# Stick-breaking attention: the second term of the scores contracted over 128 rows, the keys' low part in both halves

## The chip, the cores and the metric

The kernel runs on one core of a Trainium2 chip. The metric is the device time of one execution in microseconds (us); lower is better. Engines are named as in the profile: PE (TensorE) multiplies matrices, and PEld is its loading of the stationary operand; DVE is VectorE, ACT is ScalarE, POOL is GpSimd; SP issues the DMAs.

## The reference

One layer of a hybrid encoder on 1024 tokens with 1024 features, in float32: one input projection feeds an HGRN2 recurrence (4 heads of 128) and a stick-breaking attention (8 heads of 64); both are projected, gated, summed and projected again; then come a layer norm, a gated feed-forward part with a short causal convolution, a per-layer embedding and a second layer norm. The change concerns the attention:

```python
def stick_breaking_attention(q, k, v):
    qh = jnp.transpose(q, (0, 2, 1, 3)) * (Dh ** -0.5)
    ...
    def block(args):
        z = jnp.einsum('bhtd,bhsd->bhts', qi, kh).astype(jnp.float32)
        mask = (key_pos[None, :] < t_pos[:, None])[None, None]
        log_fail = jnp.where(mask, jax.nn.log_sigmoid(-z), 0.0)
        suffix = lax.cumsum(log_fail, axis=3, reverse=True) - log_fail
        log_w = jnp.where(mask, jax.nn.log_sigmoid(z) + suffix, 0.0)
        w = jnp.where(mask, jnp.exp(log_w), 0.0)
        return jnp.einsum('bhts,bhsd->bhtd', w, vh)
```

## The kernel before

Values are split into a high part of type fp32r and a low part, the difference (`split`: ACT copies, DVE subtracts). A product of two split matrices takes three matmuls, high by high, high by low and low by high (`mm3`, lines 93 to 95).

**Projections as filler.** The input projections are cut into small pieces (`add_fm`, `add_tm`, `add_qk0`); `fill` puts as many of them on PE between two attention steps as a balance of the remaining work says. PE's order up to the end of the input projections is that of the code (`manual_schedule`). The orders of the other engines are made by a scheduler when the program is built, and each engine works strictly in its order.

**Attention.** The 8 heads are worked in 4 pairs p; heads hd = 0 and 1 of a pair lie in partitions 0 to 63 and 64 to 127 of the projections. `q_out` (from line 316) writes for each head a tile of 128 partitions with the query's high part in one half and its low part in the other: `qsa` for hd 0, `qsb` for hd 1. `k_out` (from line 328) writes for each pair and each half h of the tokens, from the bank `psk`: `kca` and `kcb`, the high part of the keys of hd 0 and of hd 1, each in both halves of the partitions (ACT writes one half, DVE copies it to the other), and `kl`, the low part, hd 0 in the lower and hd 1 in the upper half (DVE).

`sb_weights` then makes the scores z of 128 queries with 128 to 1024 keys, in pieces of at most 512 columns:

```python
            mm(z[:, :s1 - s0], lhsT=qs[:, ts], rhs=kc[:, s0:s1], start=True, stop=False)
            mm(z[:, :s1 - s0], lhsT=qs[r, ts], rhs=kl[r, s0:s1], start=False, stop=True)
```

Line 383 contracts over 128 rows (the query's high and low part with the keys' high part), line 384 over the 64 rows `r` (the query's high with the keys' low part). Such a couple is called a pair of z matmuls here; there are 96. Behind it ACT makes two sigmoids, `f` (line 385) and `be` (386); DVE masks `f` (389) and takes its running product (391); POOL masks `be` (390) and multiplies it by `f` (393). `sb_apply` transposes `be` on PE (`tr`, 409), splits it into `wth` (ACT, 79) and `wtl` (DVE, 80), and multiplies both by the values into `av` (420); DVE adds the result to `ob` (436). `stick_breaking` runs 32 steps (4 pairs, 2 heads, 4 blocks of 256 queries), the scores of one step interleaved with the application of the step before.

`load_w` brings a weight tile by DMA and splits it (ACT line 87, DVE line 89). All larger work tiles come from the pool `gp` (24 buffers, `G(...)`); the tiles of z and `tr` from four PSUM banks (`Z`).

Of the kernel before, what the change touches and what calls it, by code (L numbers as in the profile page):

```python
# [7 lines left out]
F32 = mybir.dt.float32  # L8
F32R = mybir.dt.float32r
U8 = mybir.dt.uint8  # L10
AF = mybir.ActivationFunctionType
ALU = mybir.AluOpType
# [23 lines left out]
def layer_kernel(ctx, tc, xT, pT, w_in, w_a, w_b, w_out, w_up, w_down, w_pe, w_pg,  # L36
                 cols, conv, sbm, hgm, idn, g2r, b2r, outT, outR):
    nc = tc.nc
    cst = ctx.enter_context(tc.tile_pool(name="cst", bufs=1))
    xp = ctx.enter_context(tc.tile_pool(name="xp", bufs=16))  # L40
    wp = ctx.enter_context(tc.tile_pool(name="wp", bufs=2))
    gp = ctx.enter_context(tc.tile_pool(name="gp", bufs=24))
    hp = ctx.enter_context(tc.tile_pool(name="hp", bufs=6))
    sm = ctx.enter_context(tc.tile_pool(name="sm", bufs=4))
    
# [9 lines left out]
    def G(name, dt=F32, shape=None):  # L55
        return gp.tile(shape or [P, T], dt, tag="g", name=name)
# [19 lines left out]
    mm = nc.tensor.matmul  # L76
# [38 lines left out]
    for c, nm in ((16, "q0"), (20, "k0")):  # L115
        raw = wp.tile([P, T], F32, tag="wr", name="wr_" + nm)
        hi = wp.tile([P, T], F32R, tag="wh", name="wh_" + nm, bufs=3)
        lo = wp.tile([P, T], F32R, tag="wl", name="wl_" + nm, bufs=3)
# [64 lines left out]

    XH, XL = (lambda k: xh[k]), (lambda k: xl[k])

# [1 line left out]
    jobs = []  # L187
    state = {"job": 0, "chunk": 0, "credit": 0.0}
    CH = 0.65
# [118 lines left out]
            i += 1  # L308
        return n * CH

# [1 line left out]
    qk = [None] * 4  # L312
    v2 = [None] * 4
    ob = [None] * 4
# [13 lines left out]
    def k_out(p):  # L328
        def evac(psk, h, c):
            if h == 0:  # L330
                qk[p] = qk[p] + (G(f"kca{p}", F32R), G(f"kcb{p}", F32R), G(f"kl{p}", F32R))
            ka, kb, kl = qk[p][2:]
            nc.scalar.copy(out=ka[0:64, c], in_=psk[0:64])
            nc.vector.tensor_copy(out=ka[64:128, c], in_=ka[0:64, c].bitcast(F32))
            nc.vector.tensor_tensor(out=kl[0:64, c], in0=psk[0:64], in1=ka[0:64, c].bitcast(F32), op=ALU.subtract)
            nc.scalar.copy(out=kb[64:128, c], in_=psk[64:128])
            nc.vector.tensor_copy(out=kb[0:64, c], in_=kb[64:128, c].bitcast(F32))
            nc.vector.tensor_tensor(out=kl[64:128, c], in0=psk[64:128], in1=kb[64:128, c].bitcast(F32), op=ALU.subtract)

        return evac  # L340

# [23 lines left out]
    def sb_names(p, hd):  # L365
        r = slice(0, 64) if hd == 0 else slice(64, 128)
        ro = slice(64, 128) if hd == 0 else slice(0, 64)
        return r, ro, f"{p}{hd}"

    def sb_weights(p, hd, tb, ws):  # L370
        r, ro, nm = sb_names(p, hd)
        qa, qb, ka, kb, kl = qk[p]
        qs, kc = (qa, ka) if hd == 0 else (qb, kb)
        if hd == 0 and tb == 0:
            ob[p] = G(f"ob{p}")
        W = (tb + 1) * P
        ts = slice(tb * P, tb * P + P)
        f = G(f"f{nm}{tb}")
        be = G(f"be{nm}{tb}")
        for s0 in range(0, W, 512):  # L380
            s1 = min(s0 + 512, W)
            z = Z(f"z{nm}{tb}{s0}")
            mm(z[:, :s1 - s0], lhsT=qs[:, ts], rhs=kc[:, s0:s1], start=True, stop=False)
            mm(z[:, :s1 - s0], lhsT=qs[r, ts], rhs=kl[r, s0:s1], start=False, stop=True)  # L384
            nc.scalar.activation(f[:, s0:s1], z[:, :s1 - s0], AF.Sigmoid, scale=-0.125)
            nc.scalar.activation(be[:, s0:s1], z[:, :s1 - s0], AF.Sigmoid, scale=0.125)  # L386
            if s1 < W:
                yield
        nc.vector.tensor_tensor(out=f[:, ts], in0=f[:, ts], in1=msb[:, 1, :], op=ALU.max)
        nc.gpsimd.tensor_tensor(out=be[:, ts], in0=be[:, ts], in1=msb[:, 0, :], op=ALU.mult)  # L390
        nc.vector.tensor_tensor_scan(out=f[:, :W][:, ::-1], data0=f[:, :W][:, ::-1], data1=f[:, :W][:, ::-1],  # L391
                                     initial=1.0, op0=ALU.mult, op1=ALU.bypass)
        nc.gpsimd.tensor_tensor(out=be[:, :W - 1], in0=be[:, :W - 1], in1=f[:, 1:W], op=ALU.mult)  # L393
        ws.append(be)
        yield
# [67 lines left out]
        for _ in sb_apply(*prev):  # L463
            fill(1.3)

# [1 line left out]
    va, sga = [None] * 2, [None] * 2  # L467
    oa = [None] * 4

# [48 lines left out]
        add_fm(h, f"hq{h}", evac_q)  # L518
        add_fm(4 + h, f"hf{h}", evac_f)

    # the keys of an odd block of 128 tokens lie in falling order within every 32 of them
    def key_rows(kt, tot, m):
        k5 = kt.rearrange("p (c e t) -> p c e t", c=4, e=2)
        t5 = tot.rearrange("p (c e g) -> p c e g", c=4, e=2)
# [172 lines left out]
                    fill(left(("ia1", "ga1", "gb0", "gb3")[h]) * w / max(rest, w))  # L697
                    rest -= w

# [1 line left out]
    def split4(src, name):  # L701
        hs, ls = [], []
        for k in range(4):
# [65 lines left out]

            yproj(j, u, mh, ml, f"ya{j}", out)  # L770

# [1 line left out]
    def ln_gen(get, c0, n, emit, name):  # L773
        cs = slice(c0, c0 + n)
        nb = n // P
# [37 lines left out]
            nc.vector.tensor_tensor(out=get(j)[:, cs], in0=get(j)[:, cs], in1=pr[:, :n], op=ALU.mult)  # L813
            emit(j, cs)

# [1 line left out]
    add_qk0([w[2:] for w in wqk], (q_out(0), k_out(0)))  # L817
    add_vb(0), add_q(1), add_k(1)
    add_vb(1), add_q(2), add_k(2)
# [15 lines left out]
    R = lambda j: rt[j]  # L835
# [27 lines left out]

    X1H, X1L = (lambda k: x1h[k]), (lambda k: x1l[k])

# [1 line left out]
    def split_p(hi, lo, src):  # L867
        nc.scalar.copy(out=hi, in_=src)
        nc.gpsimd.tensor_tensor(out=lo, in0=src, in1=hi.bitcast(F32), op=ALU.subtract)
# [125 lines left out]
    with tc.manual_schedule(engines={mybir.EngineType.PE}):  # L995
# [5 lines left out]
        for i in range(4):  # L1001
            src, lst, nm = ((pT[i], pp, f"p{i}") if i < 2 else (w_pe[i - 2], pe_u, f"pe{i}"))
# [41 lines left out]
    for bs in groups:  # L1044
        last = bs is groups[-1]
# [90 lines left out]
                nc.vector.tensor_tensor(out=r, in0=r, in1=self.pr[:, :Q], op=ALU.mult)  # L1136
                y_emit(j, self.cs, how[j], cuts)

    # the last tokens lie over the partitions, with R transposed into the sums
    class Rows:  # L1140
        def __init__(self, i):
            self.i, self.nm = i, f"rw{i}"
# [170 lines left out]
```

## Time and profile before

| | us |
|---|---|
| median of 3 runs | 1756.48 (1752.68 to 1758.9) |
| the profiled execution, first to last instruction (the page gives no other time for it) | 1753.0 |
| PE busy | 1720.5 |
| DVE busy | 1025.1 |
| ACT busy | 585.7 |
| POOL busy | 373.8 |

The profiled execution is one of its own; it lies 3.5 us under the median of the runs and within their range. Neighbouring PE rows overlap, as matmuls are pipelined and their ends are modelled. What a matmul costs in a stream is the distance from its start to the next start. The attention takes the stretch from about 28 to 366 us. Its view by windows gives busy time by engine, the granted clock of PE (1.00 is full) and DMA.

### The profile page before, as it was taken

The numbers are of one execution on the slowest core, as the hardware profiler recorded it, in microseconds if no ns is written. First come the engines' busy times: TensorE is split into PE (matmuls) and PEld (weight loads), VectorE is DVE, ScalarE is ACT, GpSimd is POOL, SyncE is SP. The second block draws the span as 40 slices with busy tenths as digits, with TensorE's granted clock in tenths as the row PEclk, the third lists the DMA queues.
The fourth block names the chain that finished last, engine by engine and source line by source line (L and its number), as shares of the span: only waits on it lengthen the run. The fifth ranks groups of instructions, "written<-read, shape, count | busy, mean of one in ns | idle before, by whom it ended". The sixth has DMA issues, their size and how long they took to land.

```text
span 1753.0 us, 21252 instructions
## 1 busy us (share of the span) xinstructions
PE 1720.5 (98%) x8660; PEld 1437.9 (82%) x8660; DVE 1025.1 (58%) x1463; ACT 585.7 (33%) x899; POOL 373.8 (21%) x293
## 2 busy tenths in 40 slices
PE   8999999999999999999999999999999999999997
PEld 6778778789988888887788888888888888888896
DVE  6677867776576423347776326456456456456465
ACT  5455555542233221222345112222222222222233
POOL 0344434431012000005540102012012012012043
PEclk9999999999999999999999999999999999999998
DMA  5000000100011111111421210120120121121102
GB/s 198 25 25 25 25 25 25 37 25 29 33 37 36 49 42 55 37 60 57 148 73 36 73 36 24 49 73 24 49 72 27 47 73 34 39 72 37 60 25 96
DMA packets 26977, 88.11 MB, mean 50 GB/s; under 512 B 2944, under 2 KB 5632, under 8 KB 26880
## 3 DMA queue, kind: packets, MB, share of 16 engines
q1 hardware_dynamic: 26880, 86.76, 14.8%
q8 instruction: 68, 1.11, 0.3%
q14 instruction: 29, 0.24, 0.0%
HBM read 82.55 MB, written 4.19 MB: 49 GB/s over the span
## 4 chain that ended last, share of the span: by engine, by line
PE 87%; DVE 8%; ACT 2%; issue 1%; POOL 1%; DMA 1%; POOLq 0%; SPq 0%; ACTq 0%; DVEq 0%
PE uv L93 4%; PE uv L95 4%; PE ug L94 4%; PE ug L93 4%; PE uv L94 4%; PE ug L95 4%; PE d L94 4%; PE d L93 4%; PE d L95 4%; PE z L384 2%; PE pi_gb L95 2%; PE pi_gb L93 2%; DVE f L391 2%; PE pg L93 2%; PE pg L95 2%; PE pi_gb L94 2%
## 5 line engine op out<-in xcount | busy, mean ns | idle before, releaser
L906 POOL TENSOR_TENSOR cuv<-cuv,cug 128x1024 f32<-128x1024 f32 x21 | 50.4, 2400 | 552.2 <-DVE cug L888 552.2
L93 PE MATMUL uv<-x1h,wh_uv 128*128 128x512 f32 x352 | 136.9, 389 | 0.0
L95 PE MATMUL uv<-x1h,wl_uv 128*128 128x512 f32 x352 | 136.9, 389 | 0.0
L94 PE MATMUL uv<-x1l,wh_uv 128*128 128x512 f32 x352 | 136.9, 389 | 0.0
L93 PE MATMUL ug<-x1h,wh_ug 128*128 128x512 f32 x352 | 136.9, 389 | 0.0
L94 PE MATMUL ug<-x1l,wh_ug 128*128 128x512 f32 x352 | 136.9, 389 | 0.0
L95 PE MATMUL ug<-x1h,wl_ug 128*128 128x512 f32 x352 | 136.9, 389 | 0.0
L93 PE MATMUL d<-gh,hd 128*128 128x512 f32 x288 | 112.0, 389 | 0.0
L94 PE MATMUL d<-gl,hd 128*128 128x512 f32 x288 | 112.0, 389 | 0.0
L95 PE MATMUL d<-gh,ld 128*128 128x512 f32 x288 | 112.0, 389 | 0.0
L887 DVE SCALAR_TENSOR_TENSOR cug<-ug,cv,cug 128x1023 f32<-128x1023 f32 x21 | 26.9, 1282 | 134.1 <-ACT cug L886 134.1
L955 DVE TENSOR_TENSOR r<-r,d 128x512 f32<-128x512 f32 x144 | 94.3, 680 | 11.6 <-PE d L95 11.6
L390 POOL TENSOR_TENSOR be<-be,msb 128x128 f32<-128x128 f32 x64 | 64.4, 1007 | 170.2 <-ACT be L386 170.2
L391 DVE TENSOR_TENSOR_SCAN f<-f 128x128 f32<-128x128 f32 (+3 forms) x64 | 93.8, 1466 | 2.0
L393 POOL TENSOR_TENSOR be<-be,f 128x127 f32<-128x127 f32 (+3 forms) x64 | 77.2, 1207 | 56.3 <-DVE f L391 50.7
L886 ACT ACTIVATE cug<-ug,cv 128x1024 f32<-128x1024 f32 x21 | 25.3, 1206 | 160.3 <-PE ug L95 160.3
L95 PEld LDWEIGHTS uv<-x1h,wl_uv 128*128 128x128 f32 x352 | 66.1, 188 | 13.8
L94 PEld LDWEIGHTS ug<-x1l,wh_ug 128*128 128x128 f32 x352 | 66.1, 188 | 13.7
L94 PEld LDWEIGHTS uv<-x1l,wh_uv 128*128 128x128 f32 x352 | 66.1, 188 | 13.7
L95 PEld LDWEIGHTS ug<-x1h,wl_ug 128*128 128x128 f32 x352 | 66.1, 188 | 13.7
L93 PEld LDWEIGHTS ug<-x1h,wh_ug 128*128 128x128 f32 x352 | 66.1, 188 | 13.7
L93 PEld LDWEIGHTS uv<-x1h,wh_uv 128*128 128x128 f32 x352 | 66.1, 188 | 13.6
(462 smaller groups left out, 4617.0 us busy)
## 6 DMA issues: line engine op xcount, KB each, us to landing
wr_uv<-in_w_up SPq DMA_DIRECT2D x22, 512.0 KB, 3.2
wr_ug<-in_w_up SPq DMA_DIRECT2D x22, 512.0 KB, 3.2
wr_d<-in_w_down SPq DMA_DIRECT2D x21, 512.0 KB, 3.3
wr_wo<-in_w_out SPq DMA_DIRECT2D x16, 512.0 KB, 3.3
wr_gb<-in_w_in SPq DMA_DIRECT2D x8, 512.0 KB, 3.3
wr_gt<-in_w_in SPq DMA_DIRECT2D x8, 512.0 KB, 3.2
wr_pg<-in_w_pg SPq DMA_DIRECT2D x8, 512.0 KB, 3.3
xr<-in_xT SPq DMA_DIRECT2D x7, 512.0 KB, 8.8
```

Source lines behind the costliest of these rows:

```text
L93: mm(ps, lhsT=ah, rhs=bh, start=start, stop=False)
L94: mm(ps, lhsT=ah, rhs=bl, start=False, stop=False)
L95: mm(ps, lhsT=al, rhs=bh, start=False, stop=stop)
L384: mm(z[:, :s1 - s0], lhsT=qs[r, ts], rhs=kl[r, s0:s1], start=False, stop=True)
L390: nc.gpsimd.tensor_tensor(out=be[:, ts], in0=be[:, ts], in1=msb[:, 0, :], op=ALU.mult)
L391: nc.vector.tensor_tensor_scan(out=f[:, :W][:, ::-1], data0=f[:, :W][:, ::-1], data1=f[:, :W][:, ::-1], initial=1.0, op0=ALU.mult, op1=ALU ...
L393: nc.gpsimd.tensor_tensor(out=be[:, :W - 1], in0=be[:, :W - 1], in1=f[:, 1:W], op=ALU.mult)
L886: nc.scalar.activation(o, ps, AF.Identity, bias=cv[:, c, 3:4], scale=cv[:, c, 2:3])
L887: nc.vector.scalar_tensor_tensor(out=o[:, 1:], in0=ps[:, :T - 1], scalar=cv[:, c, 1:2], in1=o[:, 1:], op0=ALU.mult, op1=ALU.add)
L906: nc.gpsimd.tensor_tensor(out=val, in0=val, in1=gt, op=ALU.mult)
L955: nc.vector.tensor_tensor(out=R(j)[:, cs], in0=R(j)[:, cs], in1=ps[:, :n], op=ALU.add)
```

## The change

The low part of the keys gets one tile per head, `kla` and `klb`, in which it stands in both halves of the partitions; line 384 contracts over all 128 rows. The product has one more term by this (query's low by keys' low part). Each of the 8 calls of `k_out`'s `evac` so issues four subtractions on DVE in place of two. The pool `gp` gets 27 buffers; the program is built with a `dynamic_dma_scratch_size` of 1024. Comments that went are left out below.

```diff
-    gp = ctx.enter_context(tc.tile_pool(name="gp", bufs=24))
+    gp = ctx.enter_context(tc.tile_pool(name="gp", bufs=27))
...
     def k_out(p):
         def evac(psk, h, c):
             if h == 0:
-                qk[p] = qk[p] + (G(f"kca{p}", F32R), G(f"kcb{p}", F32R), G(f"kl{p}", F32R))
-            ka, kb, kl = qk[p][2:]
-            nc.scalar.copy(out=ka[0:64, c], in_=psk[0:64])
-            nc.vector.tensor_copy(out=ka[64:128, c], in_=ka[0:64, c].bitcast(F32))
-            nc.vector.tensor_tensor(out=kl[0:64, c], in0=psk[0:64], in1=ka[0:64, c].bitcast(F32), op=ALU.subtract)
-            nc.scalar.copy(out=kb[64:128, c], in_=psk[64:128])
-            nc.vector.tensor_copy(out=kb[0:64, c], in_=kb[64:128, c].bitcast(F32))
-            nc.vector.tensor_tensor(out=kl[64:128, c], in0=psk[64:128], in1=kb[64:128, c].bitcast(F32), op=ALU.subtract)
+                qk[p] = qk[p] + tuple(G(f"{nm}{p}", F32R) for nm in ("kca", "kcb", "kla", "klb"))
+            ka, kb, la, lb_ = qk[p][2:]
+
+            for hi, lo, r, ro in ((ka, la, slice(0, 64), slice(64, 128)), (kb, lb_, slice(64, 128), slice(0, 64))):
+                nc.scalar.copy(out=hi[r, c], in_=psk[r])
+                nc.vector.tensor_copy(out=hi[ro, c], in_=hi[r, c].bitcast(F32))
+                for o in (r, ro):
+                    nc.vector.tensor_tensor(out=lo[o, c], in0=psk[r], in1=hi[r, c].bitcast(F32), op=ALU.subtract)
...
-        qa, qb, ka, kb, kl = qk[p]
-        qs, kc = (qa, ka) if hd == 0 else (qb, kb)
+        qa, qb, ka, kb, la, lb_ = qk[p]
+        qs, kc, kl = (qa, ka, la) if hd == 0 else (qb, kb, lb_)
...
-            mm(z[:, :s1 - s0], lhsT=qs[r, ts], rhs=kl[r, s0:s1], start=False, stop=True)
+            mm(z[:, :s1 - s0], lhsT=qs[:, ts], rhs=kl[:, s0:s1], start=False, stop=True)
...
-    nc = bacc.Bacc("TRN2", target_bir_lowering=False, num_devices=1)
+    nc = bacc.Bacc("TRN2", target_bir_lowering=False, num_devices=1, dynamic_dma_scratch_size=1024)
```

PE's order is the same before and after, line by line. DVE's order changes around the keys. The first place is the beginning of the attention, where the first queries and keys are written (numbers at tile names are those of buffers; the running product of line 391 is named SCALAR_TENSOR_TENSOR). Before:

```order
L334 CAST kca_311<-kca_311 64x512
L335 TENSOR_TENSOR kl_313<-pi_qk_195,kca_311 64x512
L324 TENSOR_TENSOR qsb_302<-pi_qk_191,qsb_302 64x512
L334 CAST kca_311<-kca_311 64x512
L337 CAST kcb_312<-kcb_312 64x512
L338 TENSOR_TENSOR kl_313<-pi_qk_195,kcb_312 64x512
L335 TENSOR_TENSOR kl_313<-pi_qk_199,kca_311 64x512
L89 TENSOR_TENSOR wl_q_336<-wr_q_333,wh_q_335 128x512 x2
L337 CAST kcb_312<-kcb_312 64x512
L338 TENSOR_TENSOR kl_313<-pi_qk_199,kcb_312 64x512
L389 TENSOR_TENSOR f_359<-f_359,msb 128x128
```

With the change:

```order
L336 CAST kca_311<-kca_311 64x512
L338 TENSOR_TENSOR kla_313<-pi_qk_195,kca_311 64x512
L324 TENSOR_TENSOR qsb_302<-pi_qk_191,qsb_302 64x512
L338 TENSOR_TENSOR kla_313<-pi_qk_195,kca_311 64x512
L336 CAST kca_311<-kca_311 64x512
L338 TENSOR_TENSOR kla_313<-pi_qk_199,kca_311 64x512
L336 CAST kcb_312<-kcb_312 64x512
L338 TENSOR_TENSOR klb_314<-pi_qk_195,kcb_312 64x512 x2
L338 TENSOR_TENSOR kla_313<-pi_qk_199,kca_311 64x512
L89 TENSOR_TENSOR wl_q_341<-wr_q_338,wh_q_340 128x512 x2
L336 CAST kcb_312<-kcb_312 64x512
L338 TENSOR_TENSOR klb_314<-pi_qk_199,kcb_312 64x512 x2
```

Eight subtractions stand where four stood, all ahead of the first mask of `f` (line 389). The second place is where the keys of pair 1 are finished (second half of the tokens), just as the scores of that pair begin. Before:

```order
L335 TENSOR_TENSOR kl_1022<-pi_k_1036,kca_1020 64x512
L89 TENSOR_TENSOR wl_q_1144<-wr_q_1141,wh_q_1143 128x512
L337 CAST kcb_1021<-kcb_1021 64x512
L338 TENSOR_TENSOR kl_1022<-pi_k_1036,kcb_1021 64x512
L436 TENSOR_TENSOR ob_358<-av_1062,avt_1158 64x256
L389 TENSOR_TENSOR f_1168<-f_1168,msb 128x128
L391 SCALAR_TENSOR_TENSOR f_1168<-f_1168 128x128
L389 TENSOR_TENSOR f_1185<-f_1185,msb 128x128
L391 SCALAR_TENSOR_TENSOR f_1185<-f_1185 128x256
L80 TENSOR_TENSOR wtl_1209<-tr_1203,wth_1208 128x512
```

With the change:

```order
L338 TENSOR_TENSOR kla_1027<-pi_k_1044,kca_1025 64x512 x2
L89 TENSOR_TENSOR wl_q_1154<-wr_q_1151,wh_q_1153 128x512
L436 TENSOR_TENSOR ob_363<-av_1070,avt_1168 64x256
L336 CAST kcb_1026<-kcb_1026 64x512
L338 TENSOR_TENSOR klb_1028<-pi_k_1044,kcb_1026 64x512 x2
L389 TENSOR_TENSOR f_1178<-f_1178,msb 128x128
L389 TENSOR_TENSOR f_1195<-f_1195,msb 128x128
L391 SCALAR_TENSOR_TENSOR f_1178<-f_1178 128x128
L391 SCALAR_TENSOR_TENSOR f_1195<-f_1195 128x256
L80 TENSOR_TENSOR wtl_1219<-tr_1213,wth_1218 128x512
```

Two subtractions more stand ahead of the masks, the running products and the `wtl` of the step before; the small `ob` has moved ahead of the second key copy, and on ACT the copy of `avt`, which `ob` needs, has moved ahead of the copy of `kcb` in the same way. The other two pairs have the same rows.

Past the attention the orders differ in one place, around the first layer norm: the DMAs, copies and POOL subtractions that bring the embedding's input `p` and its weight `pe` (`load_g`, lines 873, 868 and 869 in both kernels) stand a few rows earlier on SP, ACT and POOL.

## Rows read from the trace of the kernel before

**Rows 1.** The page: busy time, share of the span and instructions of each engine.

```profile
PE 1720.5 (98%) x8660; PEld 1437.9 (82%) x8660; DVE 1025.1 (58%) x1463; ACT 585.7 (33%) x899; POOL 373.8 (21%) x293
```

**Rows 2.** Windows: PE, PEld, DVE, ACT, POOL busy (instructions), granted clock, DMA.

```profile
40.00:50.00 10.00, 6.98 (x45) 6.23 (x45) 6.04 (x10) 2.87 (x7) 5.62 (x6) 0.89 0.09 35
50.00:60.00 10.00, 10.00 (x67) 8.49 (x67) 5.43 (x8) 4.89 (x12) 2.24 (x3) 0.94 0.00 0
60.00:365.00 305.00, 295.87 (x1746) 238.03 (x1745) 227.32 (x313) 165.17 (x344) 128.45 (x116) 1.00 0.08 27
102.90:123.70 20.80, 20.46 (x127) 16.50 (x125) 18.57 (x26) 12.49 (x26) 11.95 (x9) 1.00 0.08 26
```

**Rows 3.** Timeline of PE around one pair of 512 columns: start, duration, line, tiles.

```profile
103.77 0.40 PE L95 MATMUL pi_k<-xh,wl_k 128*128 128x512 f32 x1
104.00 0.40 PE L383 MATMUL z<-kcb,qsb 128*128 128x512 f32 x1
104.33 0.50 PE L384 MATMUL z<-kl,qsb 64*128 64x512 f32 x1
104.75 0.50 PE L93 MATMUL pi_k<-xh,wh_k 128*128 128x512 f32 x1
105.09 0.39 PE L94 MATMUL pi_k<-xl,wh_k 128*128 128x512 f32 x1
```

**Rows 4.** Timeline of PEld at the same pair; in brackets idle time before.

```profile
104.32 0.18 PEld L384 LDWEIGHTS z<-kl,qsb 64*128 64x128 f32 x1 [0.37 <-issue]
104.75 0.19 PEld L93 LDWEIGHTS pi_k<-xh,wh_k 128*128 128x128 f32 x1 [0.25 <-issue]
```

**Rows 5.** Timeline of PE around a pair of 128 columns, and in plain projections.

```profile
75.21 0.39 PE L95 MATMUL pi_q<-xh,wl_q 128*128 128x512 f32 x1
...
76.17 0.39 PE L94 MATMUL pi_q<-xl,wh_q 128*128 128x512 f32 x1
...
100.97 0.39 PE L93 MATMUL pi_k<-xh,wh_k 128*128 128x512 f32 x1
101.20 0.40 PE L94 MATMUL pi_k<-xl,wh_k 128*128 128x512 f32 x1
```

**Rows 6.** Line 384: all its matmuls (min/median/max ns).

```profile
L384 PE MATMUL z<-kl,qsa x48: 322/466/500, 33.5 to 320.5; 64*128 64x512 f32 x24, 64*128 64x128 f32 x8, 64*128 64x256 f32 x8, 64*128 64x384 f32 x8
L384 PE MATMUL z<-kl,qsb x48: 323/464/498, 75.6 to 361.8; 64*128 64x512 f32 x24, 64*128 64x128 f32 x8, 64*128 64x256 f32 x8, 64*128 64x384 f32 x8
```

**Rows 7.** Timeline of DVE, from the first keys to the first `wtl`.

```profile
32.80 0.68 DVE L335 TENSOR_TENSOR kl<-pi_qk,kca 64x512 fp32r<-64x512 f32 x1
...
45.64 0.53 DVE L80 TENSOR_TENSOR wtl<-tr,wth 128x384 fp32r<-128x384 f32 x1
```

**Rows 8.** Timeline of PE: the wait for that `wtl`, and matmuls of 256 columns behind it.

```profile
46.22 0.45 PE L420 MATMUL av<-wtl,v 128*128 128x256 f32 x2 [1.86 <-DVE wtl L80]
...
47.98 0.41 PE L254 MATMUL pt_vb<-wl_vb,xh 128*128 128x256 f32 x1
48.19 0.41 PE L252 MATMUL pt_vb<-wh_vb,xh 128*128 128x256 f32 x1
```

**Rows 9.** Timeline of DVE at the keys of pair 1; its idle time in brackets.

```profile
107.92 0.29 DVE L389 TENSOR_TENSOR f<-f,msb 128x128 f32<-128x128 f32 x1 [0.36 <-ACT f L385]
...
112.28 0.29 DVE L389 TENSOR_TENSOR f<-f,msb 128x128 f32<-128x128 f32 x1 [0.66 <-ACT f L385]
```

**Rows 10.** Waits of PE from 60 to 366 us: total, times, longest.

```profile
PE av L420 <- DVE wtl L80: 9.1, 14, 1.3
```

**Rows 11.** Waits from 28 to 366 us and from 780 to 900 us.

```profile
ACT kca L333 <- POOL be L390: 2.2, 1, 2.2
...
PE l10pr L811 <- POOL l10ss L807: 1.3, 1, 1.3
PE l10pm L783 <- DVE l10sa L780: 0.7, 1, 0.7
```

**Rows 12.** Timeline of POOL at the first layer norm.

```profile
848.10 2.41 POOL L869 TENSOR_TENSOR lp<-wr_p,hp 128x1024 fp32r<-128x1024 f32 x1 [2.27 <-ACT hp L868]
```

## The prediction

> **What bounds the kernel now.** I read the page's busy times first: PE is busy 98% of the span and DVE 58% [rows 1]. Then the windows: in the attention, from 60 to 365 us, PE is busy 295.9 of 305 us and DVE 227.3, three quarters [rows 2]. So PE's stream sets the pace, and what an edit is worth is the distance between starts on PE. Third, PE's timeline around a pair of z matmuls: a matmul of 512 columns normally starts 0.23 us after the one before (103.77 to 104.00), but 0.33 us pass from line 383 to line 384, 0.42 us from 384 to the next and 0.34 us from that one to its successor [rows 3]. PEld shows why: the 64-row load of line 384 begins only when the matmul itself can begin, after 0.37 us in which PEld waits for nothing the profile shows; so does the 128-row load behind it, after 0.25 us [rows 4]. So each pass from 128 to 64 rows and back keeps PE from loading ahead. Last, the waits: from 60 to 366 us PE waits 14 times, 9.1 us in all, for `wtl` of DVE [rows 10]. DVE's latency is the second limit there, and this is what the change presses on.
>
> **What goes.** From the start of the matmul ahead of a pair (103.77) to that of the second one behind it (105.09) 1.32 us pass; four matmuls at 0.23 us are 0.92, so the pair costs 0.40 us too much [rows 3]. With 128 columns it is 0.96 us (75.21 to 76.17) for two matmuls of 512 and two of 128 columns [rows 5]. At 0.23 for 512 columns, my estimate for 128 is a quarter, 0.06, together 0.58: an excess of 0.38. So it hardly depends on the size, and I take 0.39 us for each of the 96 pairs [rows 6], 37.4 us in all. After the change every matmul of a pair has 128 rows; nothing else in the stream changes form, and PE's order is the same. Whether a matmul with 128 rows of `kla` runs like any other I infer from the projections around it; the bounds are 0 and 0.40 us, and I take 0.39 as the form is theirs.
>
> **What comes.** Sixteen more subtractions on DVE, 64 by 512 from PSUM, at 0.68 to 0.69 us each [rows 7]: 11.0 us. They are not hidden everywhere.
>
> - *Beginning, 28 to 46 us.* DVE works almost without a gap from the first `kl` at 32.80 to the `wtl` at 45.64, and PE waits 1.86 us for the latter [rows 7, 8]. Four added subtractions stand ahead of the first mask, so `wtl` comes 4 x 0.69 = 2.8 us later. The four pairs in this stretch gain nothing, since PE arrives earlier only to wait longer. Cost +2.8 us against before.
> - *Keys of pairs 1 to 3, 21 us each.* Pair 1's is the stretch from 102.9 to 123.7 us: DVE busy 18.57 of 20.8 us [rows 2], with gaps of 0.36 and 0.66 us for ACT's `f` [rows 9], together 1.02. Four added subtractions are 2.76 us. If the gaps take their full share, the `wtl` at its end comes 1.74 us later; if they stay, 2.76. PE waits for that `wtl` already. ACT's copy of `kcb`, too, waits for the subtraction of `kl`, now for two; the sigmoids behind it on ACT wait along. I take 1.7 us, the lower end, since DVE, later by then, finds `f` ready. The six pairs in each of these stretches again gain nothing. Cost 3 x 1.7 = +5.1 us.
> - *The rest.* 96 - 4 - 18 = 74 pairs lie elsewhere and gain 74 x 0.39 = 28.9 us.
> - *Waits that grow.* Of the 14 waits for `wtl` [rows 10] 11 lie outside the key stretches, each with a z pair between what starts its chain and its end. The part of the excess that falls behind line 384's start is 105.09 - 104.33 - 2 x 0.23 = 0.30 us [rows 3]; DVE's chain does not get faster by it, so each wait grows by so much: 11 x 0.30 = +3.3 us.
> - *Waits that appear.* The other 17 of the 32 steps show no wait; where PE comes just in time now it will wait. Between 0 and 17 x 0.30 = 5.1 us; I take the middle, +2.5.
>
> **Edits at nothing.** The three buffers pay for the new tile of each pair, of which two are alive at once. The buffer wait that shows is one of 2.2 us of ACT for POOL's `be` [rows 11]; at most this goes, or as much comes if the tiles were short. The scratch size touches nothing that moves data: the only queue with transfers of this program is SP's. At the layer norm four DMAs pass some weight loads on SP, four copies move up ACT, and four subtractions of 2.41 us move up POOL [rows 12], ahead of the rows that centre. POOL has idle time there (2.27 us before this very one); PE waits 1.3 and 0.7 us for the norm [rows 11]. At most these 2.0 us go, or one POOL subtraction is added; I take nothing, and keep -2.0 and +2.4 for the range.
>
> **Sum.** -28.9 + 2.8 + 5.1 + 3.3 + 2.5 = -15.2 us: the profiled execution of 1753.0 becomes 1737.8. The median of the runs lies 3.5 us above the profile, so the forecast is 1756.5 - 15.2 = 1741.3 us.
>
> **Rivals.**
>
> - *All of it stays.* DVE's gaps take in the key stretches and no wait grows: only the beginning costs, -28.9 + 2.8 = -26.1, that is 1730.4 us. Against it speak the 14 waits that exist. Chance 0.06.
> - *DVE takes most back.* With 12 more subtractions in 60 to 365 us DVE has 227.3 + 8.3 = 235.6 us of work. In a key stretch DVE reaches 18.57 / 20.8 = 89% of the time, which would allow 265 us and not bind. But a DVE that waits for ACT and ACT for PE may stay near its present 75%. At 79% the stretch takes 298.2 us, 6.8 less than now; with the beginning's 2.8 this gives -4, or 1752.5 us. At 78% nothing is left. Chance 0.16.
> - *The rows are not the cause.* Lines 383 and 384 load the same queries, and add into a z bank between other streams; if the late load came from that and not from the number of rows, PE gains nothing and DVE's cost stays: 2.8 + 3 x 1.7 = +7.9, 1764.4 us, slower. This decides if a pair loses less than about 10.4 / 66 = 0.16 us: the fixed costs of 2.8, 5.1 and 2.5 by the 74 pairs less the eight or so that growing waits eat. For it speaks that no pair of the program with 128 rows in both matmuls stands in this place; against it, that lines 93 and 94 also load one operand twice and start 0.23 us apart (100.97 to 101.20 [rows 5]), and that the load behind the pair, of other weights, is late as well [rows 4]. Chance 0.08. The Trainium skill (TensorE: Matmul & The Clock Gate, "Why this matters for your kernels") has a rule of this sign: a single matmul over few rows takes as long as one over 128, so that only tiles that run together gain. By that rule alone the change would save nothing on PE, and the time would be this rival's. The trace does not bear it out: at equal columns line 384's row lasts 0.50 us against 0.40 for line 383 [rows 3].
> - *The clock.* After the waits up to 46.2 us the granted clock fell from 2.4 to 1.2 GHz for part of 40 to 60 us (0.89 and 0.94 in the windows [rows 2]), with 256 columns 0.21 us apart (47.98 to 48.19 [rows 8]), nearly what 512 need at full clock. These windows lack 1.1 and 0.6 us of clock time, 1.7 us lost. If each of 14 grown waits led to the like, 14 x 1.7 = 23.8 us would go, and the sum would be +8.6, or 1765.1 us. Against it: PE's 14 waits past 60 us, the longest of 1.3 us [rows 10], left the clock at 1.00 there [rows 2]. Chance 0.04. A fall after the three key stretches alone costs 5 us and stays within the forecast's range.
>
> **How the numbers follow.** The forecast has the remaining 0.66, with its own range from 1737 (no wait appears, the norm's 2.0 gone: -15.2 - 2.5 - 2.0) to 1752 (3 x 1.06 for key stretches at 2.76, 2.6 for all new waits, 5 for three clock falls). The range to hold 8 in 10 reaches down to the first rival, 1730, and up past the second, to 1756; it leaves out the two slow ones and a little of the second. A measurement of this kernel can tell about 0.3%, 5.3 us, from no change. Faster by more: 0.64 of the forecast, 0.06 of the first rival, 0.05 of the second, 0.75. Slower by more: 0.03 of the second, 0.07 of the third, 0.02 of the fourth, 0.12. Within: 0.13.
>
> **What would show it.** Right: line 384's rows of 512 columns fall from 0.50 to about 0.40 us, PEld's idle time before them goes, and the distance over a pair of 512 columns falls from 1.32 to 0.92 us; 32 subtractions of low keys at 0.69 us; the first `av` with `wtl` starts near 49 us in place of 46.2; PE's waits for `wtl` from 60 to 366 us rise from 9.1 to about 27 us (3.3 and 2.5 from above, and 3 x (1.7 + 6 x 0.39) = 12), the longest at the keys of pairs 1 to 3; the attention ends some 15 us earlier and everything after it keeps its length. Wrong: if the distance over a pair stays above 1.2 us, the cause on PE is not the rows; if it falls and the end does not move, DVE has taken it.

## The result, and the profile after

The changed kernel takes 1737.59 us (median of 4 runs, 1735.78 to 1738.31); the kernel before, beside it, 1755.63 us (4 runs). The ratio is 0.9898, 95% interval 0.9882 to 0.9913: 18.0 us less, or 1.0%. Two later sets of runs on other chips gave 0.9908 (0.9889 to 0.9927) and 0.9903 (0.9883 to 0.9924). The forecast was 1741.3 us, 15.2 less. The profiled execution spans 1736.5 us, against 1753.0 before.

The page's busy times of the changed kernel:

```profile
PE 1688.6 (97%) x8660; PEld 1439.8 (83%) x8660; DVE 1030.3 (59%) x1479; ACT 581.1 (33%) x899; POOL 366.9 (21%) x293
```

PE runs as many instructions as before in 31.9 us less; DVE has its 16 new ones [rows 1]. The timeline of PE around a pair of 512 columns, pair 1 and head 1 as in [rows 3] (start, duration, engine, line, tiles):

```profile
100.57 0.40 PE L95 MATMUL pi_k<-xh,wl_k 128*128 128x512 f32 x1
100.81 0.40 PE L383 MATMUL z<-kcb,qsb 128*128 128x512 f32 x1
101.04 0.39 PE L384 MATMUL z<-klb,qsb 128*128 128x512 f32 x1
101.27 0.39 PE L93 MATMUL pi_k<-xh,wh_k 128*128 128x512 f32 x1
101.50 0.40 PE L94 MATMUL pi_k<-xl,wh_k 128*128 128x512 f32 x1
```

And PEld at the same pair, to be read against [rows 4]:

```profile
100.58 0.19 PEld L383 LDWEIGHTS z<-kcb,qsb 128*128 128x128 f32 x1
100.81 0.19 PEld L384 LDWEIGHTS z<-klb,qsb 128*128 128x128 f32 x1
101.05 0.19 PEld L93 LDWEIGHTS pi_k<-xh,wh_k 128*128 128x128 f32 x1
```

Every start is now 0.23 or 0.24 us behind the one before: 0.93 us from line 95 to line 94, where 1.32 passed. Line 384 lasts 0.39 us in place of 0.50. The bracket with PEld's 0.37 us of idle time is gone, since each load runs beside the matmul ahead of it.

DVE pays for it. Groups of line 338 on DVE, 28 to 300 us (count, then total us and mean ns of one, then idle time before them):

```profile
L338 DVE TENSOR_TENSOR klb<-pi_k,kcb 64x512 fp32r<-64x512 f32 x12 | 8.3, 694 | 0.2
L338 DVE TENSOR_TENSOR kla<-pi_k,kca 64x512 fp32r<-64x512 f32 x12 | 8.2, 683 | 0.2
L338 DVE TENSOR_TENSOR klb<-pi_qk,kcb 64x512 fp32r<-64x512 f32 x4 | 2.8, 694 | 0.1
L338 DVE TENSOR_TENSOR kla<-pi_qk,kca 64x512 fp32r<-64x512 f32 x4 | 2.7, 683 | 0.1
```

That is 32 subtractions, 22.0 us, of which half is new. PE's waits from 60 to 366 us (total, times, longest):

```profile
PE av L420 <- DVE wtl L80: 21.1, 17, 2.8
PE tr L409 <- DVE wtl L80: 1.8, 3, 0.7
PE tr L409 <- POOL be L393: 0.3, 1, 0.3
```

23.2 us, where 9.1 stood [rows 10]. Two waits can be seen alone. The first lies ahead of these, at the end of the beginning of the attention, where PE started this `av` at 46.22 us before [rows 8]; the second is the longest of those above, at the end of pair 1's key stretch. Both from PE's timeline, the cause in brackets:

```profile
48.41 0.69 PE L420 MATMUL av<-wtl,v 128*128 128x256 f32 x2 [1.62 <-DVE wtl L80]
...
122.22 0.50 PE L420 MATMUL av<-wtl,v 128*128 128x256 f32 x2 [2.78 <-DVE wtl L80]
```

The windows of the changed kernel (PE, PEld, DVE, ACT, POOL busy, then the granted clock) over the beginning and over that key stretch:

```profile
40.00:50.00 10.00, 5.40 (x30) 4.77 (x29) 8.18 (x15) 2.87 (x7) 5.62 (x6) 0.75 0.15 52
50.00:60.00 10.00, 10.00 (x77) 9.82 (x75) 4.52 (x8) 4.85 (x12) 2.04 (x3) 0.91 0.01 2
...
99.60:122.30 22.70, 18.88 (x127) 16.72 (x126) 21.99 (x30) 12.09 (x26) 9.13 (x9) 1.00 0.07 24
```

In the key stretch DVE is busy 21.99 of 22.7 us, 97%, and PE 18.88. Before it was the other way round: PE 20.46 of 20.8 us, DVE 18.57 [rows 2]. So here the bound has passed from PE to DVE.

The granted clock tells one more thing. Windows of the changed kernel behind the keys of pairs 1, 2 and 3 (columns as above):

```profile
120.00:130.00 10.00, 7.79 (x51) 7.74 (x52) 5.14 (x12) 1.99 (x6) 1.24 (x2) 0.83 0.00 1
124.00:126.00 2.00, 2.00 (x11) 2.00 (x11) 0.58 (x2) 0.15 (x1) 0.00 (x0) 0.50 0.00 0
200.00:210.00 10.00, 7.25 (x59) 6.96 (x58) 6.23 (x15) 2.87 (x8) 1.63 (x3) 1.00 0.11 42
280.00:290.00 10.00, 7.25 (x48) 7.24 (x48) 5.33 (x11) 1.90 (x5) 1.24 (x2) 0.83 0.08 31
```

Behind pair 1's and pair 3's wait the clock fell to 0.50, that is from 2.4 to 1.2 GHz, for a while: 0.83 over 10 us, 1.7 us lost each time. Behind pair 2's it did not, though that wait is as long (2.75 us at 203.14). The two later profiles of the changed kernel have 0.83, 1.00 and 0.83 in the same three windows. From 60 to 1720 us the kernel before had no window of 10 us under 1.00.

**Where the time went.** PE's order is the same in both kernels, so each of its instructions can be set against itself. The table gives how much earlier or later PE arrives at the end of a stretch than it did, relative to the stretch's start (times of the kernel before, us). The last row runs to the end of the span, and the sum includes the first 29 us.

| stretch | change | PE alone | DVE alone | buffers alone |
|---|---|---|---|---|
| beginning, 29 to 46.3 | +2.40 | 0.00 | +2.28 | +0.15 |
| 46.3 to 102.9 | -5.54 | -6.86 | -1.77 | -0.49 |
| keys of pair 1, to 123.75 | +1.72 | -0.84 | +2.50 | +0.07 |
| to 186.3 | -4.10 | -5.58 | -0.55 | +0.05 |
| keys of pair 2, to 207.05 | +1.73 | -0.64 | +2.22 | 0.00 |
| to 270.2 | -6.03 | -6.10 | -0.32 | -0.57 |
| keys of pair 3, to 291.1 | +1.60 | -0.87 | +2.36 | +0.02 |
| to 366 | -5.77 | -7.16 | -0.26 | -0.25 |
| total by 402, attention done | -13.9 | -27.2 | +6.6 | -1.6 |
| 780 to 900, first layer norm | -1.66 | +0.02 | -1.67 | -1.65 |
| 900 to 1719 | +0.56 | 0.00 | +0.42 | +0.57 |
| total at the end of the span | -16.5 | -28.9 | +5.5 | -2.6 |

The last three columns are the experiments below. In two places the differences come from the granted clock and not from the work done there. The first is the tail between 1719 us and the end. The kernel before has a fall of the clock there, near the end, which the profile of the changed kernel has not. Windows (columns as above) of the kernel before, then of the changed kernel at the same work:

```profile
1720.00:1730.00 10.00, 8.65 (x41) 7.28 (x40) 5.34 (x14) 2.27 (x6) 5.36 (x6) 0.83 0.18 66
1705.00:1715.00 10.00, 8.66 (x52) 7.33 (x51) 6.96 (x19) 3.50 (x9) 5.80 (x7) 1.00 0.19 71
```

That is 1.7 us, about what the profiles differ by. Of those below, PE alone lacks this fall too and DVE alone and the buffers alone have it; what decides it is not shown.

The second place is the row from 46.3 us. The clock falls around the first `av` with `wtl` in every profile of this table, but not at the same place. Windows from that `av` to 60 us in the kernel before, the changed kernel, PE alone and DVE alone:

```profile
46.20:60.00 13.80, 13.78 (x88) 12.27 (x89) 5.85 (x9) 5.26 (x13) 3.17 (x4) 0.88 0.00 1
48.40:60.00 11.60, 11.59 (x82) 11.41 (x82) 4.94 (x9) 5.22 (x13) 2.96 (x4) 0.86 0.00 1
46.80:60.00 13.20, 13.17 (x105) 12.95 (x106) 7.33 (x12) 6.28 (x16) 5.96 (x5) 1.00 0.01 1
48.70:60.00 11.30, 11.27 (x79) 9.89 (x80) 4.82 (x9) 5.26 (x13) 2.88 (x4) 1.00 0.01 1
```

The first two lose about 1.7 us behind that `av`; in the halves the fall was over when PE came out of its wait. So about 1.7 us of -6.86 and nearly all of -1.77 in that row come from where the fall lay.

### The profile page after: what moved, and what is told of

Its sections match the earlier page's. It is cut to its first block, busy times and chain, and to the rows that moved or that the text cites. A ratio compares the mean times of both kernels' runs of the same rounds, so it can differ in the third digit from the quotient of the medians.

```text
span 1736.5 us, 21248 instructions
## 1 busy us (share of the span) xinstructions
PE 1688.6 (97%) x8660; PEld 1439.8 (83%) x8660; DVE 1030.3 (59%) x1479; ACT 581.1 (33%) x899; POOL 366.9 (21%) x293
## 4 chain that ended last, share of the span: by engine, by line
PE 84%; DVE 11%; ACT 2%; issue 2%; POOL 1%; DMA 0%; POOLq 0%; SPq 0%; ACTq 0%; DVEq 0%
PE uv L95 4%; PE uv L93 4%; PE uv L94 4%; PE ug L94 4%; PE ug L93 4%; PE ug L95 4%; PE d L93 4%; PE d L95 4%; PE d L94 4%; DVE f L391 3%; PE pi_gb L95 2%; PE pi_gb L93 2%; PE pi_gb L94 2%; PE pg L93 2%; PE pg L95 2%; PE pi_gt L94 2%
## 5 line engine op out<-in xcount | busy, mean ns | idle before, releaser
L390 POOL TENSOR_TENSOR be<-be,msb 128x128 f32<-128x128 f32 x64 | 54.3, 849 | 149.5 <-ACT be L386 149.1
```

## The experiments

### The two halves of the change, each alone

DVE's half: the changed kernel with line 384 as it was.

```diff
-            mm(z[:, :s1 - s0], lhsT=qs[:, ts], rhs=kl[:, s0:s1], start=False, stop=True)
+            mm(z[:, :s1 - s0], lhsT=qs[r, ts], rhs=kl[r, s0:s1], start=False, stop=True)
```

> The changed kernel, but line 384 contracts over the 64 rows r again: the 16 added subtractions, the new tiles and the three buffers stay, half of each low tile is written and not read. Left out: the term of the query's low with the keys' low part. Theory (the gain is the number of rows on PE, the cost is DVE's latency at the beginning and at the keys of pairs 1 to 3): the distance over a pair of 512 columns stays 1.32 us as before, and DVE's cost of 2.4 + 3 x 1.7 = 7.5 us shows alone, so +5 to +9 us against before, 1761 to 1765 us (less up to 2 us if the buffers help at the norm). Rival (DVE's added work is hidden by other work, and the growth of PE's waits in the changed kernel is only lost gain): within 2 us of before, 1754 to 1758 us. Rival (the gain comes from the separate tiles or the buffers, not from the rows): near the changed kernel, 1738 us.

Measured: 1761.01 us (1759.14 to 1762.64) against 1754.16, ratio 1.0036 (1.0023 to 1.0048): 6.9 us slower. The excess of a pair stays at 0.40 to 0.41 us, and PE's waits for `wtl` from 60 to 366 us rise:

```profile
PE av L420 <- DVE wtl L80: 14.2, 17, 2.2
```

PE's half: the kernel before, with a second term over 128 rows that needs no new tile.

```diff
-            mm(z[:, :s1 - s0], lhsT=qs[r, ts], rhs=kl[r, s0:s1], start=False, stop=True)
+            mm(z[:, :s1 - s0], lhsT=qs[:, ts], rhs=kc[:, s0:s1], start=False, stop=True)
```

> The kernel before, with one edit: line 384 contracts over 128 rows, with kca or kcb as its moving operand in place of kl, so nothing is added on DVE. Left out: the low part of the keys (kl is written and not read; the first term is added twice). Theory: the whole excess of 0.39 us goes from every pair and no cost comes; the stretches without keys gain 21 us as in the changed kernel, the key stretches about 1.5 us each in place of losing 1.7, the beginning 0 in place of losing 2.4: 25 to 29 us less than before, 1727 to 1731 us. Rival (DVE's latency, not its added work, limits what PE can gain in the key stretches and at the beginning): no better than the changed kernel by more than 3 us, 1735 to 1738 us. Rival (the rows are not the cause): 1754 to 1758 us.

Measured: 1727.48 us (1726.41 to 1727.82), ratio 0.9842 (0.9828 to 0.9856): 26.7 us faster. PE's waits from 60 to 366 us:

```profile
PE av L420 <- DVE wtl L80: 16.2, 17, 1.4
PE tr L409 <- POOL be L393: 0.4, 1, 0.4
```

So both halves exist, with the signs that the prediction gave them. At the end of the attention they don't add up: -27.2 and +6.6 would be -20.6, and the change has -13.9. The table shows where. At the beginning and in the three key stretches, where PE waits for DVE's added work, the halves give 7.0 us (2.28, then 1.66, 1.58 and 1.49) and the change 7.5, nearly the same: DVE's work costs 9.4 us there under a slow PE, and 9.8 under a fast one (change less PE alone). The gap lies in the four other stretches: -25.7 and -2.9 for the halves, -21.4 for the change. This is no waiting for DVE's added work, which has been done there for long; it has the clock's pattern. Neither half lost anything of the clock from 60 us to the end of the attention. The changed kernel lost 1.7 us each behind pairs 1 and 3, where it falls 1.5 and 1.4 us short of PE alone, and nothing behind pair 2, where it is 0.1. In the first of the four stretches each half is about 1.7 us ahead by where its fall lay, which need not be the change's doing: the version with zeros and 23 buffers below, which adds no work to DVE, has 0.88 from 46.2 to 60 us and gains 5.40 us in this stretch, the changed kernel 5.54. And a faster PE makes its own waits: they grow from 9.1 to 16.6 us without one added DVE instruction. In the key stretches PE alone saves only 0.6 to 0.9 us where six pairs hold 2.3.

### Is it the 64 rows, or the change to them and back?

The kernel before, with line 383 over 64 rows as well.

```diff
-            mm(z[:, :s1 - s0], lhsT=qs[:, ts], rhs=kc[:, s0:s1], start=True, stop=False)
+            mm(z[:, :s1 - s0], lhsT=qs[r, ts], rhs=kc[r, s0:s1], start=True, stop=False)
```

> The kernel before, with line 383 also contracted over the 64 rows r: both matmuls of a pair have 64 rows, the neighbours 128. Left out: the term of the query's low with the keys' high part. Theory 1 (what costs is each pass between 128 and 64 rows, in either direction): 383 starts 0.33 us after a 512-column neighbour, 384 0.23 us after 383, the neighbour 0.42 us after 384, its successor 0.34 us on; the excess of a pair stays 0.40 us and the time within 4 us of before, 1752 to 1760 us. Theory 2 (a matmul of 64 rows is itself slow, by 0.2 us or more each): 0.33 us or more also between 383 and 384, an excess of 0.6 to 0.8 us, 20 to 35 us slower, 1775 to 1791 us.

Measured: 1754.86 us (1752.75 to 1756.3), ratio 1.0000 (0.9991 to 1.001): no change, with twice as many matmuls over 64 rows. PE's timeline around the same pair:

```profile
102.58 0.40 PE L95 MATMUL pi_k<-xh,wl_k 128*128 128x512 f32 x1
102.90 0.49 PE L383 MATMUL z<-kcb,qsb 64*128 64x512 f32 x1
103.24 0.39 PE L384 MATMUL z<-kl,qsb 64*128 64x512 f32 x1
103.56 0.50 PE L93 MATMUL pi_k<-xh,wh_k 128*128 128x512 f32 x1
103.90 0.40 PE L94 MATMUL pi_k<-xl,wh_k 128*128 128x512 f32 x1
```

And PEld's, with the idle time before each load:

```profile
102.90 0.18 PEld L383 LDWEIGHTS z<-kcb,qsb 64*128 64x128 f32 x1 [0.37 <-issue]
103.01 0.19 PEld L384 LDWEIGHTS z<-kl,qsb 64*128 64x128 f32 x1
103.56 0.19 PEld L93 LDWEIGHTS pi_k<-xh,wh_k 128*128 128x128 f32 x1 [0.37 <-issue]
```

The distance from line 95 to line 94 is 1.32 us, as with one such matmul. Line 384, behind another of 64 rows, lasts 0.39 us, no longer than one over 128, and its load starts 0.11 us after the load ahead of it. The late loads have moved with the border: to line 383 on the way in and to line 93 on the way out. So a matmul over 64 rows costs nothing of its own that shows in the sum; an excursion from 128 rows to 64 and back costs 0.40 us, whether it holds one matmul or two. The split over the single steps (0.32, 0.34, 0.32, 0.34) was not the one I expected; the sum was.

The rule of the Trainium skill that the prediction weighed (TensorE: Matmul & The Clock Gate, "Why this matters for your kernels") is right in this: a matmul over few rows takes as long as one over 128. Line 384 lasts 0.39 us here, as one over 128 rows does. The rule fails as a forecast, as it has no price for the border. The Trainium skill (TensorEngine Tiling (Array Packing), "Key Properties") says that changing the tiling mode drains TensorE. The trace agrees if a slice of 64 rows counts as another mode, which is not shown: in these rows loads wait at both borders, 0.37 us each, and nowhere else.

### The three buffers

The kernel before with the changed sizes alone.

```diff
-    gp = ctx.enter_context(tc.tile_pool(name="gp", bufs=24))
+    gp = ctx.enter_context(tc.tile_pool(name="gp", bufs=27))
...
-    nc = bacc.Bacc("TRN2", target_bir_lowering=False, num_devices=1)
+    nc = bacc.Bacc("TRN2", target_bir_lowering=False, num_devices=1, dynamic_dma_scratch_size=1024)
```

> The kernel before with gp of 27 buffers and the scratch size of the change, nothing else. Theory as predicted (the buffers are worth nothing in the attention): the attention ends at the same time within 0.5 us. What the changed kernel gained at the first layer norm (1.7 us between 780 and 900 us, by earlier loads of p and pe) comes with the buffers if they cause it: 1753 to 1756 us in all. Rival (the buffers take waits for tiles away in the attention, part of the 18 us): the attention ends 2 us or more earlier, 1750 us or less.

Measured: 1751.49 us (1750.45 to 1752.86), ratio 0.9983 (0.9974 to 0.9992): 2.7 us faster by the medians. One part is the layer norm's 1.65 us, the gain that the changed kernel has there too; 0.57 us of it is lost again by 1719 us. PE's waits from 780 to 900 us are the same rows in this kernel and in the changed one; here those of this kernel:

```profile
PE l10pr L811 <- POOL l10ss L807: 1.1, 1, 1.1
PE wo L95 <- DVE wl_wo L89: 0.6, 1, 0.6
```

Before, the first was 1.3 us, the second 1.1, and a third one of 0.7 us stood beside them [rows 11]. So the rows that the change moved on POOL, ACT and SP (and a few of DVE and ACT near 650 us, a second place beside the norm, where nothing is gained) had moved because of the changed sizes, and they brought a gain. The scratch size was not tried apart, but the version with zeros and 23 buffers below has it too and gains only 0.21 us at the norm.

PE is also 1.6 us ahead by the end of the attention, more than the theory allowed. The changed kernel does not owe this to the buffers. 0.6 us of it arise ahead of 29 us, where the three profiles of the changed kernel differ by 0.9 us among themselves. Most of the rest is four waits for `wtl` that are each 0.26 to 0.28 us shorter, and the orders of all engines are those of the kernel before up to 650 us. At all four DVE's mask of `f` and POOL's product of `be` start almost together. The last of them, two lines of the kernel before, then two with the buffers:

```profile
340.59 0.86 POOL L393 TENSOR_TENSOR be<-be,f 128x383 f32<-128x383 f32 x1
340.63 0.97 DVE L389 TENSOR_TENSOR f<-f,msb 128x128 f32<-128x128 f32 x1 [0.38 <-ACT f L385]
339.32 0.29 DVE L389 TENSOR_TENSOR f<-f,msb 128x128 f32<-128x128 f32 x1 [0.32 <-ACT f L385]
339.34 0.99 POOL L393 TENSOR_TENSOR be<-be,f 128x383 f32<-128x383 f32 x1
```

Where DVE comes first, its mask takes 0.29 us in place of 0.91 to 0.97, and the running product behind it 1.77 in place of 1.37. The changed kernel and PE alone have DVE first at all four, 0.28 to 0.41 us ahead of POOL, with 27 buffers as with 24; so there the buffers have nothing left to turn round.

### The second half made by another engine

One subtraction per head stays on DVE; the second half is a copy of the first, from SBUF, on POOL or on ACT.

```diff
-                for o in (r, ro):
-                    nc.vector.tensor_tensor(out=lo[o, c], in0=psk[r], in1=hi[r, c].bitcast(F32), op=ALU.subtract)
+                nc.vector.tensor_tensor(out=lo[r, c], in0=psk[r], in1=hi[r, c].bitcast(F32), op=ALU.subtract)
+                nc.gpsimd.tensor_copy(out=lo[ro, c], in_=lo[r, c].bitcast(F32))
```

On POOL:

> The changed kernel with the second half of each low tile made by a copy of the first on POOL in place of a second subtraction on DVE; nothing is left out. Theory: DVE's added 11 us are gone, the start and the key stretches cost what POOL's copies delay the first scores: POOL's own products of be stand behind the copies; between the changed kernel and PE alone, 1728 to 1735 us. Rival (any added step between keys and scores costs as much as DVE's): 1736 to 1740 us.

Measured: 1731.19 us (1729.89 to 1732.53), ratio 0.9870 (0.9853 to 0.9887). The key stretches cost 0.15 to 0.21 us in place of 1.6 to 1.7; the beginning still costs 2.09.

On ACT, with `nc.scalar.copy` in the place of `nc.gpsimd.tensor_copy`:

> The changed kernel with the second half of each low tile made by a copy of the first on ACT; nothing is left out. ACT's copies of 64 x 512 take 0.58 us, and the copy has to wait for DVE's subtraction with the sigmoids behind it on ACT. Theory: better than the changed kernel in the key stretches by up to the 1.4 us per half that DVE loses, less what ACT's waiting adds; 1729 to 1737 us. Rival (ACT, in order, holds up the sigmoids and so the chain to wtl as much as DVE did): 1737 to 1742 us.

Measured: 1732.39 us (1731.06 to 1733.7), ratio 0.9877 (0.9859 to 0.9894). Here the beginning costs 0.21 us, and the key stretches 1.17 to 1.30. Each engine has room where the other has none. The clock bears out its share: on POOL, PE waits 1.94 us behind the keys of pairs 1 and 3, the clock falls behind both, and from there to the next keys PE gains 4.07 and 5.81 us, as in the change (4.10, 5.77). On ACT it falls nowhere from 60 to 360 us, and PE gains 5.58 and 7.26, as PE alone does (5.58, 7.16). The changed kernel ran on the same chip:

> The changed kernel once more, on the same chip as the versions above, so that they can be compared with it: 1735 to 1739 us.

It took 1738.07 us (1737.49 to 1739.05). So what DVE takes back is due to DVE's time, and making the second half elsewhere returns 5.7 to 6.9 us of it.

### No second half at all: zeros

The 64 rows that line 384 has to add need not hold the low keys. With zeros there the product is that of the kernel before. Four tiles of low keys stay for the whole attention, two by two for alternate pairs. POOL writes the zeros once, and each pair writes its own half alone.

```diff
+    klz = []
+    for i in range(2):
+        pair = tuple(cst.tile([P, T], F32R, name=f"kl{nm}z{i}") for nm in "ab")
+        nc.gpsimd.memset(pair[0][64:128].bitcast(F32), 0.0)
+        nc.gpsimd.memset(pair[1][0:64].bitcast(F32), 0.0)
+        klz.append(pair)
...
-                qk[p] = qk[p] + tuple(G(f"{nm}{p}", F32R) for nm in ("kca", "kcb", "kla", "klb"))
+                qk[p] = qk[p] + (G(f"kca{p}", F32R), G(f"kcb{p}", F32R)) + klz[p % 2]
...
-                for o in (r, ro):
-                    nc.vector.tensor_tensor(out=lo[o, c], in0=psk[r], in1=hi[r, c].bitcast(F32), op=ALU.subtract)
+                nc.vector.tensor_tensor(out=lo[r, c], in0=psk[r], in1=hi[r, c].bitcast(F32), op=ALU.subtract)
```

Since the four tiles lie outside `gp`, the pool had 23 buffers in this run.

> The changed kernel with the other half of each low tile zero in place of a second subtraction: four fixed low tiles (hd 0 and 1, pairs of even and odd number) whose unused halves are cleared once on POOL before the keys are written; line 384 contracts over 128 rows, DVE subtracts 16 times as before, gp has 23 buffers, the same memory in all. The term of the query's low with the keys' low part is left out, as in the kernel before. Theory (rows on PE give, DVE's second subtractions take): the attention ends 25 to 28 us before that of the kernel before, as with PE alone; 1724 to 1729 us, some 10 us less than the changed kernel. Rival (part of the changed kernel's loss against PE alone comes from the tiles and their waits, not from DVE): 1731 to 1737 us.

Measured: 1735.31 us (1734.77 to 1735.83), ratio 0.9893 (0.9877 to 0.991): a miss by 6 us and more, in the rival's range but not by the rival's cause. The attention ended 26.7 us earlier, as foreseen, but far behind it, from 1560 to 1733 us, PE has a wait that neither kernel had:

```profile
PE dl L94 <- DVE gl L80: 6.1, 1, 6.1
```

It took back 7.2 us between 1600 and 1719 us. The suspect was the pool of 23, so the same with the four tiles from `gp` and 27 buffers:

```diff
-        pair = tuple(cst.tile([P, T], F32R, name=f"kl{nm}z{i}") for nm in "ab")
+        pair = tuple(G(f"kl{nm}z{i}", F32R) for nm in "ab")
...
-    gp = ctx.enter_context(tc.tile_pool(name="gp", bufs=23))
+    gp = ctx.enter_context(tc.tile_pool(name="gp", bufs=27))
```

> e9 with its four low tiles taken from gp, with 27 buffers as in the changed kernel, so that their memory is free again after the attention. Left out as in e9: the term of the query's low with the keys' low part. In e9 the attention ended 26.7 us before that of the kernel before, and 6.1 us went at one wait of the last down-projection (PE for gl of DVE), where the kernel before and the changed one do not wait. Theory (that wait comes from gp having one buffer less than before): the wait goes, the attention ends 25 to 28 us earlier, the norm gains its 1 to 2 us: 1724 to 1728 us. Rival (the wait comes from the fixed tiles or the order): 1731 to 1736 us.

Measured: 1724.71 us (1723.71 to 1728.3), ratio 0.9828 (0.9809 to 0.9846) against 1754.16: 29.4 us faster than the kernel before. The page's busy times and the windows over the beginning and a key stretch:

```profile
PE 1683.6 (98%) x8660; PEld 1436.1 (83%) x8660; DVE 1020.1 (59%) x1463; ACT 581.0 (34%) x899; POOL 375.7 (22%) x297
```

```profile
40.00:50.00 10.00, 7.89 (x49) 7.47 (x50) 6.01 (x10) 3.46 (x9) 5.62 (x6) 0.83 0.07 27
50.00:60.00 10.00, 10.00 (x83) 9.82 (x82) 7.29 (x11) 5.93 (x16) 3.78 (x4) 1.00 0.00 0
...
99.00:122.00 23.00, 21.45 (x160) 20.13 (x159) 18.91 (x27) 12.14 (x28) 8.72 (x8) 1.00 0.07 24
```

DVE has its 1463 instructions again and PE leads in the key stretch. The wait of 6.1 us is gone, so it came with the smaller pool; the place of the four tiles changed along with it. The changed kernel on the same chip:

> The changed kernel on the same chip as e10, for the comparison: 1735 to 1739 us.

It took 1738.16 us (1737.43 to 1740.53), so the version with zeros beats it by 13.4 us. This is close to the 13.3 us by which the changed kernel trails PE alone at the end of the attention.

## Why the prediction was right

Forecast 15.2 us less, measured 18.0; 1737.59 us lies well inside the range. By its steps:

- **What goes.** A pair of 512 columns went from 1.32 to 0.93 us. By distances between starts, as in the prediction, the mean excess of a pair is now 0.004 to 0.016 us at 256 to 512 columns. At 128 columns 0.11 us stay. There, in the changed kernel, the loads of the pair's second matmul and of the two behind it start 0.11 us apart (75.00, 75.11, 75.22), further than the 0.06 us that a quarter of 512 columns was put at; that the loads set the pace there is inferred. The cause, inferred from late loads, was shown by the run with both lines over 64 rows.
- **Rows are not the cause.** This rival falls with the same rows.
- **The beginning**: +2.8 forecast, +2.40 measured, with the first such `av` at 48.41 us where 49 was said.
- **The key stretches**: +1.7 each forecast, +1.72, +1.73 and +1.60 measured. DVE is busy 97% of pair 1's stretch and waits for `f` in none of the three, as the choice of the lower end had it. But the number is right by two misses that offset each other. The six pairs were to gain nothing, and PE alone gains 0.6 to 0.9 us. DVE's work was to cost 1.7, and alone it costs 2.2 to 2.5, though DVE waits for `f` nowhere in that run either: in pair 1's stretch its busy time grows by 3.5 us (18.73 to 22.22), where four subtractions are 2.76.
- **The rest**: -28.9 + 3.3 + 2.5 = -23.1 us forecast; -5.54 - 4.10 - 6.03 - 5.77 = -21.4 measured. The 11 waits outside the key stretches grew from 8.1 to 11.5 us, +3.4 where +3.3 was said, by 0.1 to 0.8 us each and not evenly by 0.30. The waits that were to appear, +2.5, did not: all new waits for `wtl` lie in the key stretches. In their place stand the two falls of the clock behind the keys, 1.5 and 1.4 against PE alone, which the sum did not hold. The remaining 1.2 us are not taken apart; the pairs of 128 columns keep 0.11 us each.
- **Waits for `wtl` from 60 to 366 us**: about 27 us forecast, 22.9 measured. The longest are at the keys, as said.
- **The clock.** It was a rival with a fall behind each of 14 waits. That did not come, but the weak form did which the prediction left inside the range at 5 us: falls behind two of three key stretches, 1.7 us each. The argument that waits past 60 us left the clock at 1.00 rested on waits of up to 1.3 us [rows 10]; with 2.8 it no longer held each time.
- **Edits at nothing.** The term was 0, with -2.0 kept for the norm in the range. The norm gained 1.66 us, of which 0.56 was lost again later. The 2.0 counted two waits of PE; a third, 1.1 us for `wl_wo`, fell to 0.6 as well. The buffers alone also gained in the attention, but not by a tile that came sooner, and in the changed kernel no such gain shows.
- **The sum**, by places: the attention ends 13.9 us earlier where 15.2 was said (1.3 too much). Behind it the profile gains 2.6 us that were forecast as nothing: 1.66 at the norm less 0.56 later, by the buffers, and about 1.6 of the tail, where the kernel before lost as much to a fall of the clock. The medians gain 1.5 us more than the profile. So the mechanism held, but the total is this near the forecast partly by luck, because misses of either sign offset each other.
- **DVE takes most back.** From 60 us to the attention's end DVE is now busy past the 79% at which that rival had it stop:

```profile
60.00:351.00 291.00, 268.06 (x1752) 241.78 (x1751) 235.78 (x325) 161.14 (x344) 120.78 (x117) 0.99 0.09 28
```

235.78 of 291 us are 81%. In these profiles the changed kernel is 13.3 us short of PE alone's 27.2 at the end of the attention, about half: 9.8 where it waits for DVE's work, 2.9 behind pairs 1 and 3, where the clock fell, and 1.3 in the stretch from 46.3 us, where the fall at the beginning lay differently, less 0.7 in the first 29 us.

What stays open: what decides whether and where the clock falls behind a wait, and why DVE's own cost in a key stretch is larger than its added subtractions.

## What to carry to other kernels

Read the distance between starts, not durations, at each place where the number of contracted rows changes in a stream of matmuls, and count the borders: a short contraction between long ones is dear here, and zeros in the unused rows cost one write for the whole run. If the filling of those rows needs work per use, put it on the engine that has room in that very stretch; here the kernel with zeros is 13.4 us faster than the one in which DVE makes the same half. When a change makes the leading engine faster, added work on the second engine can cost more than it does alone: here the waits cost the same (9.4 and 9.8 us), but the clock fell behind two of them. So test the two halves apart and together, and look at the granted clock before a difference of one or two us between profiles is put down to the change.

## What the runs showed of the hardware that was not expected

- Between two matmuls over 64 rows no load waits (it starts 0.11 us behind the load ahead of it); only the passages between 128 and 64 rows cost, 0.40 us for both together, at one matmul inside or two. Each passage shows in two steps, 0.32 and 0.34 us where 0.23 is usual.
- Pairs of 128 columns keep an excess of 0.11 us with all rows at 128. The prediction took their full 0.38 as gained.
- The clock's fall does not follow from the length of one wait: it came behind PE's waits of 2.78 and 2.75 us (pairs 1 and 3) and not behind one of 2.75 (pair 2) in the changed kernel, behind two of 1.94 us with the copy on POOL, and not behind 2.17 us with DVE's half alone.
- DVE's mask of 128x128 took 0.29 us where it started just ahead of a product on POOL, and 0.91 to 0.97 us where it started just behind it.
